# An encoder layer's MLP in two phases through DRAM, with Strassen's seven products in the up-projection

## The chip, the cores and the metric

The kernel runs on one core of one Trainium2 chip. Five engines work in parallel, each through its own queue of instructions in a fixed order: TensorE (PE: matmuls and transposes; PEld is its weight load), VectorE (DVE), ScalarE (ACT), GpSimd (POOL) and SyncE (SP), which issues nearly all DMAs here. An instruction that waits for a semaphore holds up everything behind it on its engine. The metric is the device time of one execution in microseconds, less is better; the figure is the median of several runs.

## The reference

The layer takes 16 meta tokens and 2048 tokens of width 1024 through a mixer (attention beside a state-space model) and an MLP. The part that the change touches, in float32:

```python
h = h + rms_norm(mix @ w_out[i], g_post_mix[i])
m = rms_norm(h, g_pre_mlp[i]) @ w_mlp_up[i]          # 2048 x 1024 @ 1024 x 4096
m = jnp.square(jax.nn.relu(m)) @ w_mlp_down[i]       # 2048 x 4096 @ 4096 x 1024
h = h + rms_norm(m, g_post_mlp[i])
```

## The kernel before

Float32 accuracy comes from three matmuls in place of one. `split` (L118 to L120) makes of a float32 tensor a high part (an ACT cast, L119) and a low part (a DVE subtraction, L120), and every product is high x high + high x low + low x high. A matmul has 128 rows and 128 columns of weights and streams 512 columns.

The stages on PE: projections, then attention with the state-space model and the gated unit beside it (until about 1600 us), the output projection (16 tiles of 128 tokens) and the MLP from 1818 us to the end. The kernel is written in a tile framework that orders each engine's queue itself, by priorities, and sets the waits from the tiles' pools: a pool with one buffer makes the next writer wait for the last reader. DMAs on SP go round eight completion lanes, so that each also waits for the one eight before it.

Output projection, `out_tile` (L1177 to L1212): per tile 48 matmuls (`op`, L1196), scaled and added by ACT (`ot`, L1200) and DVE (`o`, L1201), a row norm (`rstd_of`, small GpSimd instructions L125, L126), the residual, and a write of the tile to DRAM (`HD`, L1208). For tiles 0 to 7 follow the norm before the MLP (`hn`, L1165 to L1167) and, two tiles later, eight transposes (`hT`, L1174) whose splits lie in SBUF as `hh`, `hl`. The scratch buffer `ot`/`jk` has one copy, so a tile's chain must end before the next tile's first `ot` can be written.

MLP: two halves of 1024 tokens (`ct`). For each 256 of the 4096 inner columns, `up` (L1242 to L1263) loads 512 KB of weights twice and splits them; PE makes 24 matmuls for each 128 columns x 512 tokens (L1257), ACT takes the Relu (L1260), DVE squares (L1261), and the result is split into `mh`, `ml`, which stay in SBUF. `d_load` (L1265 to L1277) fetches the down weights through one buffer (`draw`), and `down` (L1279 to L1294) multiplies the block that was made one step earlier, and adds it into the accumulator `acc` (DVE, L1294). Up blocks and down blocks alternate on PE, one step apart, so that neither waits. Tiles 8 to 15 are normalised and transposed within the MLP, at the end of the first half. `finish` does the last norm and writes the output.

Of the kernel before, what the change touches and what calls it, by code (L numbers as in the profile page):

```python
# [9 lines left out]
F32 = mybir.dt.float32  # L10
# [12 lines left out]
# 2*pi cut into parts of few bits, so that a whole number times a part is exact.  # L23
# [18 lines left out]
# 1 / 10000 ** (2 j / 32) as float32 arithmetic gives it  # L42
# [9 lines left out]
def hymba_layer_kernel(  # L52
# [41 lines left out]
    # per group of 16 channels: row 16 (7 - i) + h, column = chunk of 8 tokens; the meta tokens' two chunks apart  # L94
# [9 lines left out]
    HD = mk(dram, [NT, 128, D], "HD")  # L104

# [35 lines left out]
        # a -> a - 2 pi round(a / 2 pi), exactly but for the last rounding  # L141
# [59 lines left out]
    # w_ukv columns are per head [64 nope | 64 v]: kept as [nope of all heads | v of all heads]  # L201
# [47 lines left out]
    # the meta tokens come second  # L249
# [62 lines left out]
    def proj(t, xhl):  # L312
        rows = 128 if t < NT else NM
        # kv latent and shared rotary key
# [55 lines left out]
    def u_T(t, un):  # L370
        # u, feature-major, to its chunks
# [103 lines left out]
    # what the first head doesn't wait for  # L475
# [7 lines left out]
    # ------------------------------------------------------------------ attention: its pools  # L483
# [34 lines left out]
    def head_units(h):  # L518
        # loads and splits of a head's keys and values, in small steps
# [71 lines left out]
    def attend(n, side):  # L591
        # side: for each key tile, the small steps of other work that go with it
# [15 lines left out]
        for t in range(NK):  # L608
# [12 lines left out]
            else:  # L621
                # rows 0..: high parts, 32..: low parts, 64..: high parts
# [23 lines left out]
    # the last queries' projections, beside the first maxima  # L646
# [11 lines left out]
    # ------------------------------------------------------------------ S5  # L658
# [23 lines left out]
    def exp_exact(pool, a, tag):  # L682
        # (exp(a), exp(a) - 1), both to float32's accuracy
# [33 lines left out]
    def s5_params():  # L717
        with pool("s5a", 1, "right") as ap:
# [60 lines left out]
            # exp(a) cos - 1 = (exp(a) - 1) - 2 exp(a) sin(half)^2, exp(a) sin = 2 exp(a) sin(half) cos(half)  # L779
# [11 lines left out]
            # (lam_bar - 1) / lam  # L791
# [22 lines left out]
            # powers  # L814
# [21 lines left out]
    def s5_all():  # L836
        yield from s5_params()
        s5z = s5.enter_context(pool("s5z", 1, "right"))
        # S5 states before each chunk: forward rows in rising, backward rows in falling order of chunks
# [38 lines left out]
            # C lam^n: forward rows n = 0..8, backward rows n = 8..0  # L878
# [21 lines left out]
        for b in range(NB5):  # L900
# [5 lines left out]
            for gg in range(S5B):  # L906
# [12 lines left out]
                # lags: forward 0..7 in slots 7..14, backward 7..0 in slots 0..7  # L919
# [11 lines left out]
                if gg == 1:  # L931
                    # two groups side by side in column tiles
# [283 lines left out]
    for t in range(NT):  # L1216
        nxt = operands(t + 1) if t + 1 < NT else None
        hn = out_tile(t, ops)
        if last and last[0][0] == t - 2:
            hn_T(*last.pop(0))  # L1220
# [146 lines left out]
```

## Time and profile before

| | |
|---|---|
| three runs | 3228.26, 3229.64, 3230.37 us, median 3229.64 |
| profiled execution: span | 3227.4 us |
| granted PE clock, mean | 0.982 |
| output projection's first matmul to the MLP's first | 1586.0 to 1818.2 us |
| MLP on PE | 1818.2 to 3219.6 us |

The page of the profile gives the busy time of each engine, 40 equal slices of the span, the chain of work that ended last, and the costliest groups of instructions. Other views give instructions in time, groups by line, and busy times in chosen windows. A line number in them is that of the kernel listed above, and a name like `up<-hh,uh` is output and inputs. In a group's row the numbers behind the bar are total busy us and mean ns of one, then the engine's idle time before them and what ended it.

### The profile page before, as it was taken

The page shows a single profiled execution, that of the slowest core. Times are in us where ns is not written, and L with a number is a line of the kernel's source. Part 1 is how long each engine was busy: PE and PEld are TensorE (multiplying, and loading weights), DVE is VectorE, ACT ScalarE, POOL GpSimd, SP SyncE. Part 2 cuts the span into 40 slices and gives each one's busy share as a digit, 9 for nine tenths or more (in the row PEclk, how much of TensorE's full clock was granted, in tenths as well). Part 3 has the DMA queues.
Part 4 walks back from the last instruction along what each step waited for, and adds up shares of the span by engine and source line. Part 5 has one row for each costly group of instructions (what it writes and reads, how often), then busy time and mean ns, then how long its engine had stood idle before and what let it go on. Part 6 is the DMA issues. An engine that isn't in the chain of part 4 may idle for free.

```text
span 3227.4 us, 41607 instructions
## 1 busy us (share of the span) xinstructions
PE 3097.5 (96%) x14839; PEld 2480.8 (77%) x14839; DVE 1863.1 (58%) x2943; ACT 1477.8 (46%) x2735; POOL 911.1 (28%) x2107
## 2 busy tenths in 40 slices
PE   6999988989999999999889999999999999999999
PEld 6899955656777766688767888888888888888887
DVE  6333278767888866675367534444446644444445
ACT  4333356988777799964444331122113422111122
POOL 4222166775888876600023100000000100000001
PEclk8999999999999999999989999999999999999999
DMA  4232231211000122231245411111112411111113
GB/s 150 64 85 75 64 82 30 59 43 31 26 14 26 26 73 85 68 122 46 71 133 141 150 47 45 52 52 49 50 46 79 157 52 46 53 46 46 46 46 104
DMA packets 228495, 216.52 MB, mean 67 GB/s; under 512 B 32336, under 2 KB 193488, under 8 KB 228288
## 3 DMA queue, kind: packets, MB, share of 16 engines
q1 hardware_dynamic: 226240, 212.17, 22.3%
q8 instruction: 116, 1.90, 0.2%
q10 hardware_dynamic: 1792, 1.57, 0.2%
q14 instruction: 91, 0.75, 0.1%
q0 software_dynamic: 256, 0.14, 0.0%
HBM read 160.34 MB, written 53.41 MB: 66 GB/s over the span
## 4 chain that ended last, share of the span: by engine, by line
PE 65%; ACT 4%; DMA 3%; issue 2%; DVE 2%; POOL 1%; SPq 0%; DVEq 0%; POOLq 0%; ACTq 0%
PE dn L1289 22%; PE up L1257 22%; PE z L1072 2%; PE s L612 2%; PE s L614 2%; PE s L613 2%; PE X L604 2%; PE X L605 2%; PE X L606 2%; PE mxp L566 2%; PE op L1196 2%; ACT zh L119 1%; DMA rb<-RD 1%; PE y L1008 1%; ACT ph L616 1%
## 5 line engine op out<-in xcount | busy, mean ns | idle before, releaser
L1294 DVE TENSOR_TENSOR acc<-dn,acc 128x512 f32<-128x512 f32 x464 | 316.9, 690 | 223.5 <-PE dn L1289 223.4
L620 DVE TENSOR_TENSOR pl<-s,ph 128x512 fp32r<-128x512 f32 x512 | 350.2, 686 | 160.2 <-ACT s L619 157.1
L616 ACT ACTIVATE ph<-s 128x512 fp32r<-128x512 f32 (+1 forms) x544 | 323.4, 595 | 171.1 <-PE s L614 155.9
L1257 PE MATMUL up<-hl,uh 128*128 128x512 f32 x1024 | 398.6, 389 | 0.0
L1257 PE MATMUL up<-hh,uh 128*128 128x512 f32 x1024 | 398.5, 389 | 0.0
L1257 PE MATMUL up<-hh,ul 128*128 128x512 f32 x1024 | 398.4, 389 | 0.0
L1289 PE MATMUL dn<-dh,ml 128*128 128x512 f32 x1008 | 392.3, 389 | 0.0
L1289 PE MATMUL dn<-dl,mh 128*128 128x512 f32 x1008 | 392.2, 389 | 0.0
L1289 PE MATMUL dn<-dh,mh 128*128 128x512 f32 x1008 | 392.0, 390 | 0.0
L567 DVE TENSOR_REDUCE mx<-mxp 128x1 f32<-128x512 f32 x512 | 343.0, 684 | 58.1 <-PE mxp L566 54.7
L119 ACT CAST dh<-raw 128x1024 fp32r<-128x1024 f32 x63 | 66.2, 1051 | 642.0 <-PE dn L1289 495.7
L125 POOL TENSOR_SCALAR rs_v<-ss 128x1 f32<-128x1 f32 (+1 forms) x98 | 24.3, 248 | 995.9 <-ACT hn L1165 662.8
L619 ACT ACTIVATE s<-s 128x512 f32<-128x512 f32 x512 | 304.0, 594 | 0.8
L612 PE MATMUL s<-ql,kh 96*128 96x512 f32 (+1 forms) x544 | 226.1, 416 | 14.3 <-ACT ZS L930 4.9
L1261 DVE TENSOR_TENSOR r<-r 128x512 f32<-128x512 f32 x128 | 88.3, 690 | 247.5 <-ACT r L1260 247.5
L604 PE MATMUL X<-pl,vt 128*65 128x512 f32 x512 | 208.9, 408 | 21.3 <-DVE pl L620 20.7
L1257 PEld LDWEIGHTS up<-hh,ul 128*128 128x128 f32 x1024 | 192.3, 188 | 40.1
L1257 PEld LDWEIGHTS up<-hl,uh 128*128 128x128 f32 x1024 | 192.2, 188 | 39.9
L1257 PEld LDWEIGHTS up<-hh,uh 128*128 128x128 f32 x1024 | 192.2, 188 | 39.9
L1289 PEld LDWEIGHTS dn<-dl,mh 128*128 128x128 f32 x1008 | 189.3, 188 | 39.4
L1289 PEld LDWEIGHTS dn<-dh,ml 128*128 128x128 f32 x1008 | 189.2, 188 | 39.5
L1289 PEld LDWEIGHTS dn<-dh,mh 128*128 128x128 f32 x1008 | 189.2, 188 | 39.2
(411 smaller groups left out, 6799.1 us busy)
## 6 DMA issues: line engine op xcount, KB each, us to landing
raw<-in_w_mlp_up_dram SPq DMA_DIRECT2D x64, 512.0 KB
raw<-in_w_mlp_down_dram SPq DMA_DIRECT2D x64, 512.0 KB
xt<-in_x_dram SPq DMA_DIRECT2D x32, 512.0 KB
ht<-HD SPq DMA_DIRECT2D x24, 512.0 KB
ug<-UD SPq DMA_DIRECT2D x32, 256.0 KB
HD<-o SPq DMA_DIRECT2D x16, 512.0 KB
out_dram<-jk SPq DMA_DIRECT2D x32, 256.0 KB
kvraw<-QD SPq DMA_DIRECT2D x32, 192.0 KB
```

Source lines behind the costliest of these rows:

```text
L119: S.copy(out=h, in_=src)
L566: T.matmul(out=p, lhsT=qs[n][0][0:96, j * 128:(j + 1) * 128], rhs=kh[0:96, b * 512:(b + 1) * 512])
L567: V.reduce_max(out=mxs[n][:, j, b:b + 1], in_=p, axis=AX.X)
L604: T.matmul(out=X[:65], lhsT=v[:, t, 0:65], rhs=pl_, start=(t == 0), stop=False)
L612: T.matmul(out=s[:m], lhsT=kh[0:96, cs], rhs=ql, start=True, stop=False)
L616: S.activation(out=ph_[:m], in_=s[:m], func=AF.Exp, scale=SCALE)
L619: S.activation(out=s, in_=s, func=AF.Exp, scale=SCALE)
L620: V.tensor_tensor(out=pl_, in0=s, in1=f(ph_), op=ALU.subtract)
L1257: T.matmul(out=p, lhsT=a[:, k], rhs=c[:, k, cs], start=(k == 0 and i == 0), stop=(k == 7 and i == 2))
L1261: V.tensor_tensor(out=r, in0=r, in1=r, op=ALU.mult)
L1289: T.matmul(out=p, lhsT=a[:, ts_], rhs=c[:, hs], start=(n == 0 and w == 0), stop=(n == len(keys) - 1 and w == 2))
L1294: V.tensor_tensor(out=acc[:, i, hs], in0=p, in1=acc[:, i, hs], op=ALU.add)
```

## The change

The MLP is done in two phases. Phase 1 makes the whole up-projection of all 2048 tokens, takes the squared Relu and stores it in DRAM (`MD`, 32 MB of float32). Phase 2 reads it back and does the whole down-projection.

In phase 1 the product of 256 inner columns and 1024 tokens (a pair) is seen as 2 x 2 blocks: 1024 input features in halves, columns in halves of 128, tokens in halves of 512. Strassen's algorithm (in Winograd's form) makes the four output blocks with seven block products instead of eight, and sums of blocks before and after. A block product is 12 matmuls.

- The token side's sums (`B11`, `B21`, `B22`, `T1` to `T4`) are made once per half of the tokens, in `hn_T`, on the transposed tiles: DVE makes `t1`, `t3`, GpSimd `t2` and `T4`. They are written to DRAM (`TBD`) per 128 tokens, in runs of 512 bytes, 256 KB each: two writes for a tile i < 4 of a half, two reads and five writes for one with i >= 4. `hn` is now made for all 16 tiles in the output projection, and transposed one tile later.
- `t_load` brings each of the seven back, 1 MB, through one buffer (`traw`) and splits it into `T{n}h`, `T{n}l`. For the first half that is done before the first pair, for the second within pair 15, after each of its products; the places of `T{n}` are the same for both halves.
- The weight side's sums are made per pair by GpSimd (`up_prep`), from a load of 1 MB, and split into a pool of nine places.
- The sums behind the products: two products are added onto others in PSUM (`first=False`), the rest goes by `p1`, `u2`, `u3` on ACT and DVE. The square moves from DVE to ACT.
- Phase 2 takes blocks of 512 inner columns, four parts of 512 tokens each; `m_load` fetches and splits the stored part, `d_load` the weights; the accumulator holds all 16 tiles.

The core of the diff (comments that the change removes and loads that stay alike are left out):

```diff
-        if t < 8:
-            hn = W["e1"].tile([128, D], F32, tag="hn", name="hn", bufs=2)
-            hn_norm(o, hn, jk)
-            return hn
+        hn = W["e1"].tile([128, D], F32, tag="hn", name="hn", bufs=2)
+        ss = sm.tile([128, 1], F32, tag="ss", name="ss")
+        S.activation(out=jk, in_=o, func=AF.Square, accum_out=ss)
+        r = rstd_of(ss, D)
+        V.scalar_tensor_tensor(out=hn, in0=o, scalar=r, in1=gpr, op0=ALU.mult, op1=ALU.mult)
+        return hn
...
+        if i < 4:
+            for n, p in ((B11, ps[0]), (B21, ps[1])):
+                b = t4(f"b{n}")
+                S.copy(out=b, in_=p)
+                put(n, b)
+        else:
...
+            S.copy(out=b22, in_=ps[1])
+            V.tensor_tensor(out=t1, in0=ps[0], in1=b11, op=ALU.subtract)
+            V.tensor_tensor(out=t3, in0=b22, in1=ps[0], op=ALU.subtract)
+            G.tensor_tensor(out=t2, in0=b22, in1=t1, op=ALU.subtract)
+            G.tensor_tensor(out=b21, in0=t2, in1=b21, op=ALU.subtract)
+            for n, b in ((B22, b22), (T1, t1), (T3, t3), (T2, t2), (T4, b21)):
+                put(n, b)
...
+        G.tensor_tensor(out=s1, in0=a21, in1=a22, op=ALU.add)
+        G.tensor_tensor(out=s2, in0=s1, in1=a11, op=ALU.subtract)
+        G.tensor_tensor(out=s3, in0=a11, in1=a21, op=ALU.subtract)
+        G.tensor_tensor(out=s4, in0=a12, in1=s2, op=ALU.subtract)
+        for src in (a11, s2, a12, s3, s1, a22, s4):
+            h = apool.tile([128, 4, 128], F32R, tag="ah", name="ah")
+            l = apool.tile([128, 4, 128], F32R, tag="al", name="al")
+            split(src, h, l)
+            yield h, l
...
+    def t_load(ct, n):
+        raw = tst.tile([128, 4, 512], F32, tag="traw", name="traw")
+        Y.dma_start(out=raw, in_=TBD[ct, n])
...
+        for k in range(0, 4, 2):
+            split(raw[:, k:k + 2], h[:, k:k + 2], l[:, k:k + 2])
...
+    def relu2(c, src, n, odd, half):
+        S.activation(out=c, in_=src, func=AF.Relu)
+        S.activation(out=c, in_=c, func=AF.Square)
+        ct, j = n // NP, n % NP
+        Y.dma_start(out=MD[ct, 2 * j + odd][:, half * 512:(half + 1) * 512], in_=c)
...
+        prod(pA, mine[0], TB[B11])
+        S.copy(out=p1, in_=pA)
+        step(0)
+        prod(pB, mine[1], TB[T2])
+        V.tensor_tensor(out=u2, in0=pB, in1=p1, op=ALU.add)
+        step(1)
+        prod(pA, mine[2], TB[B21], False)
+        relu2(rt(), pA, n, 0, 0)
+        step(2)
+        prod(pB, mine[3], TB[T3], False)
+        V.tensor_tensor(out=u3, in0=pB, in1=p1, op=ALU.add)
+        step(3)
+        prod(pE, mine[4], TB[T1])
...
+        prod(pF, mine[5], TB[T4])
...
+        prod(pE, mine[6], TB[B22], False)
...
-    mpool = ctx.enter_context(pool("mD", 4, "right"))
-    dpool = ctx.enter_context(pool("dD", 3, "right"))
-    draw = ctx.enter_context(pool("draw", 1, "right"))
-    acc = mk(accp, [128, 8, 1024], "acc")
+    mpool = ctx.enter_context(pool("mD", 8, "right"))
+    dpool = ctx.enter_context(pool("dD", 8))
+    draw = ctx.enter_context(pool("draw", 2))
+    acc = mk(accp, [128, NT, 1024], "acc")
...
+            raw = draw.tile([128, 512], F32, tag="mraw", name="mraw")
+            Y.dma_start(out=raw, in_=MD[c // 2, b * FB + q][:, (c % 2) * 512:(c % 2) * 512 + 512])
```

Three places in the engines' queues. First PE from the last output tile to the MLP, before: the last matmuls of the output projection, and the first of up, whose inputs `hh`, `hl` were split long ago (`woh`, `wol` are the output projection's weights).

```order
L1196 MATMUL op_20873<-wol_16801,sh_20722 128x512
L1196 MATMUL op_20873<-woh_16800,sl_20723 128x512
L1257 MATMUL up_20932<-hh_19056,uh_20926 128x512
L1257 MATMUL up_20932<-hh_19056,ul_20927 128x512
L1257 MATMUL up_20932<-hl_19057,uh_20926 128x512
```

The same place on PE now: the transposes of tiles 14 and 15 stand between, and the first product reads `T0h`, an operand that comes back from DRAM.

```order
L1186 MATMUL op_21113<-wol_16803,sh_20926 128x512
L1186 MATMUL op_21113<-woh_16802,sl_20927 128x512
L1221 MATMUL hT_21147<-ident_82,hn_21019 128x128 x4
L1221 MATMUL hT_21152<-ident_82,hn_21019 128x128 x4
L1221 MATMUL hT_21213<-ident_82,hn_21139 128x128 x4
L1221 MATMUL hT_21218<-ident_82,hn_21139 128x128 x4
L1303 MATMUL pA_21314<-T0h_21260,ah_21185 128x512
```

Nothing of up stands ahead of the last tile's transposes any more. Second, PE further on, at the end of pair 0's fifth product (`pE`) and the beginning of pair 1 (`pA_21465`).

```order
L1303 MATMUL pE_21316<-T4l_21293,ah_21201 128x512
L1303 MATMUL pE_21316<-T4h_21292,al_21202 128x512
L1303 MATMUL pF_21317<-T5h_21300,ah_21205 128x512
L1303 MATMUL pA_21465<-T0h_21260,ah_21344 128x512
L1303 MATMUL pA_21465<-T0l_21261,ah_21344 128x512
```

One matmul that reads operand 5 stands ahead of pair 1, which reads operands 0 and 1 first. Third, SP at the start of phase 1: `t1` to `b2` are tile 15's five writes (L1215), `traw` the operands' loads (L1290), the `MD` rows pair 0's results, `raw` a weight load.

```order
L1215 DMA TBD_80<-t1_21228 512x1x128
L1290 DMA traw_21258<-TBD_80 128x2048
L1215 DMA TBD_80<-b22_21227 512x1x128
L1215 DMA TBD_80<-t3_21230 512x1x128
L1215 DMA TBD_80<-t2_21229 512x1x128
L1215 DMA TBD_80<-b2_21224 512x1x128
L1290 DMA traw_21266<-TBD_80 128x2048
L1290 DMA traw_21274<-TBD_80 128x2048
L1290 DMA traw_21282<-TBD_80 128x2048
L1314 DMA MD_81<-r_21377 128x512
L1290 DMA traw_21290<-TBD_80 128x2048
L1251 DMA raw_21636<-in_w_mlp_up_dram 128x8x256
```

Before, SP held at that place the loads of down weights and of the MLP's residual, with nothing of the hidden state; now the first load of an operand stands behind the last tile's first write. At the end of phase 1 SP holds the first loads of phase 2 behind the last store.

```order
L1314 DMA MD_81<-r_26159 128x512
L1386 DMA raw_26188<-in_w_mlp_down_dram 128x1024
L1396 DMA mraw_26194<-MD_81 128x512
L1386 DMA raw_26200<-in_w_mlp_down_dram 128x1024
L1396 DMA mraw_26206<-MD_81 128x512
```

In before there was no such seam: up and down alternated.

More of the change, by code (lines that the diff above doesn't have):

```diff
@@ new lines, in hymba_layer_kernel, with up_prep @@
+    NP = FF // 256
+    def up_prep(n):
+        j = n % NP
+        raw = wraw.tile([128, 8, 256], F32, tag="raw", name="raw")
+        Y.dma_start(out=raw, in_=w_mlp_up[0, :, j * 256:(j + 1) * 256].rearrange("(k p) f -> p k f", p=128))
+        a11, a12, a21, a22 = raw[:, 0:4, 0:128], raw[:, 4:8, 0:128], raw[:, 0:4, 128:256], raw[:, 4:8, 128:256]
+        st = [wraw.tile([128, 4, 128], F32, tag=f"st{i}", name=f"st{i}", bufs=1) for i in range(4)]
+        s1, s2, s3, s4 = st
+        G.tensor_tensor(out=s1, in0=a21, in1=a22, op=ALU.add)
[7 more added lines that the diff above has]
+            yield h, l
@@ new lines, in hymba_layer_kernel, with prod @@
+    upr = up_.enter_context(pool("upr", 6, "right"))
+    TB = {}
+    def t_load(ct, n):
+        raw = tst.tile([128, 4, 512], F32, tag="traw", name="traw")
+        Y.dma_start(out=raw, in_=TBD[ct, n])
+        h = mk(tb, [128, 4, 512], f"T{n}h", F32R)
+        l = mk(tb, [128, 4, 512], f"T{n}l", F32R)
+        for k in range(0, 4, 2):
+            split(raw[:, k:k + 2], h[:, k:k + 2], l[:, k:k + 2])
+        TB[n] = (h, l)
+    def prod(p, left, right, first=True):
+        ah, al = left
+        bh, bl = right
+        for k in range(4):
+            for i, (a, b) in enumerate(((ah, bh), (ah, bl), (al, bh))):
+                T.matmul(out=p, lhsT=a[:, k], rhs=b[:, k], start=(first and k == 0 and i == 0),
+                         stop=(k == 3 and i == 2), skip_group_check=not first)
@@ new lines, in ut, with up_pair, step, rt @@
+    def ut(name):
+        return upu.tile([128, 512], F32, tag=name, name=name)
+    def relu2(c, src, n, odd, half):
[3 more added lines that the diff above has]
+        Y.dma_start(out=MD[ct, 2 * j + odd][:, half * 512:(half + 1) * 512], in_=c)
+    def up_pair(n):
+        ct = n // NP
+        mine = facs[:]
+        facs.clear()
+        nxt = up_prep(n + 1) if n + 1 < 2 * NP else iter(())
+        def step(i):
+            f = next(nxt, None)
+            if f is not None:
+                facs.append(f)
+            if n == NP - 1:
+                t_load(1, i)
+        def rt():
+            return upr.tile([128, 512], F32, tag="r", name="r")
+        pA, pB, pE, pF = pa("pA"), pa("pB"), pa("pE"), pa("pF")
+        p1, u2, u3 = ut("p1"), ut("u2"), ut("u3")
+        prod(pA, mine[0], TB[B11])
[11 more added lines that the diff above has]
+        prod(pE, mine[4], TB[T1])
+        r = rt()
+        V.tensor_tensor(out=r, in0=pE, in1=u3, op=ALU.add)
+        relu2(r, r, n, 1, 1)
+        step(4)
+        prod(pF, mine[5], TB[T4])
+        r = rt()
+        V.tensor_tensor(out=r, in0=u3, in1=pF, op=ALU.subtract)
+        relu2(r, r, n, 1, 0)
+        step(5)
+        prod(pE, mine[6], TB[B22], False)
+        r = rt()
+        V.tensor_tensor(out=r, in0=pE, in1=u2, op=ALU.add)
+        relu2(r, r, n, 0, 1)
+        step(6)
@@ new lines, in finish, with down @@
+            Y.dma_start(out=ov[t // 8, t % 8][:, hs], in_=jk[:, hs])
+    def down(b, t, ms, ds):
+        ts_ = slice((t % 4) * 128, (t % 4) * 128 + 128)
+        for half in range(2):
+            hs = slice(half * 512, (half + 1) * 512)
+            p = pa("dn")
+            for q in range(FB):
+                mh, ml = ms[q]
+                dh, dl = ds[q]
+                for w, (a, c) in enumerate(((mh, dh), (mh, dl), (ml, dh))):
+                    T.matmul(out=p, lhsT=a[:, ts_], rhs=c[:, hs], start=(q == 0 and w == 0),
+                             stop=(q == FB - 1 and w == 2))
+            if b == 0:
+                S.copy(out=acc[:, t, hs], in_=p)
+            else:
+                V.tensor_tensor(out=acc[:, t, hs], in0=p, in1=acc[:, t, hs], op=ALU.add)
@@ new lines, in hymba_layer_kernel @@
+    parts = [(b, c) for b in range(NB) for c in range(4)]
+    ds, ms = [], []
+    for d, m in zip(d_load(0), m_load(0, 0)):
+        ds.append(d)
+        ms.append(m)
+    nds = []
+    for n, (b, c) in enumerate(parts):
+        nm = m_load(*parts[n + 1]) if n + 1 < len(parts) else iter(())
+        if c == 0:
+            nd = d_load(b + 1) if b + 1 < NB else iter(())
+        nms = []
+        for i in range(4):
+            t = 4 * c + i
+            down(b, t, ms, ds)
+            if b == NB - 1:
+                finish(t)
+            nms.extend(x for x in [next(nm, None)] if x)
+            if i == 1:
+                nds.extend(x for x in [next(nd, None)] if x)
+        ms = nms
+        if c == 3:
+            ds, nds = nds, []
```

155 lines of the change are left out of this document (56 added, 99 removed).

## The prediction

> **What bounds the kernel now.** I read the page first: busy time, the slices, the chain that ended last.
>
> ```profile
> span 3227.4 us, 41607 instructions
> PE 3097.5 (96%) x14839; PEld 2480.8 (77%) x14839; DVE 1863.1 (58%) x2943; ACT 1477.8 (46%) x2735; POOL 911.1 (28%) x2107
> PE   6999988989999999999889999999999999999999
> PE 65%; ACT 4%; DMA 3%; issue 2%; DVE 2%; POOL 1%; SPq 0%; DVEq 0%; POOLq 0%; ACTq 0%
> ```
>
> TensorE is the busiest engine, and the last 18 slices, from 1775 us on, hold the MLP and read 9. A busy PE alone doesn't say that nothing else ends last, so the chain of waits from 1600 us on comes next (start, length, what).
>
> ```profile
> 1806.89 11.30 PE op L1196 x48
> 1818.20 43.57 PE up L1257 x192
> 1861.77 21.77 PE dn L1289 x96
> 1883.54 21.77 PE up L1257 x96
> ...
> 2471.33 0.87 PE hT L1174 x8
> 2472.20 2.76 PE dn L1289 x12
> ...
> 3175.40 44.15 PE dn L1289 x192
> 3219.57 0.70 DVE acc L1294
> ```
>
> Every piece from 1818.20 to 3219.57 is a matmul, each starting where the one before ended: the MLP is 1401.4 us of TensorE without a hole. 21.77 / 96 = **0.2268 us per matmul**, the price that a matmul taken away returns. (The page's 389 ns per matmul is start to end of one in a pipeline, which overlaps the next.) The other resources have room there, as the table of windows shows (PE, PEld, DVE, ACT, POOL busy, then clock, DMA share, GB/s):
>
> ```profile
> 2000.00:2600.00 600.00, 600.00 (x2679) 497.14 (x2678) 306.71 (x418) 150.24 (x238) 19.53 (x36) 1.00 0.22 67
> 1640.00:1660.00 20.00, 13.42 (x56) 10.60 (x55) 14.62 (x19) 8.55 (x16) 3.99 (x8) 0.83 0.49 154
> 1680.00:1740.00 60.00, 58.69 (x284) 48.00 (x282) 46.73 (x61) 31.11 (x55) 17.43 (x38) 1.00 0.53 147
> 2060.60:2062.40 1.80, 1.80 (x10) 1.49 (x9) 0.00 (x0) 0.00 (x0) 0.00 (x0) 1.00 0.87 280
> 2072.60:2074.90 2.30, 2.30 (x12) 1.91 (x11) 0.16 (x1) 0.60 (x1) 0.00 (x0) 1.00 0.77 223
> ```
>
> So what is taken from PE in the MLP comes back in full, unless the new form makes PE wait. PE is dense in before because everything it reads there already lies in SBUF; the sum below is about the places where the change sends it through DRAM.
>
> **1. Matmuls removed: -87.1 us.** Up had 2 halves x 32 x 2 x 24 = 3072 matmuls; seven products of 12 per pair, 32 pairs, make 2688. 384 x 0.2268 = 87.1. Down keeps 3072. A pair is 84 matmuls, 19.05 us, a product 2.72 us.
>
> **2. The steady pair: 0.** What stands beside those 19.05 us, priced by these groups (busy, mean ns):
>
> ```profile
> L119 ACT CAST mh<-r 128x512 fp32r<-128x512 f32 x128 | 79.2, 619 | 67.8 <-DVE r L1261 67.8
> L1260 ACT ACTIVATE r<-up 128x512 f32<-128x512 f32 x128 | 76.2, 595 | 284.8 <-PE up L1257 284.8
> L120 DVE TENSOR_TENSOR ml<-r,mh 128x512 fp32r<-128x512 f32 x128 | 88.1, 689 | 42.6 <-ACT mh L119 42.6
> L860 POOL TENSOR_TENSOR ul<-ug,uh 128x516 fp32r<-128x516 f32 x32 | 42.2, 1319 | 35.3 <-ACT uh L859 19.3 <-PE s L614 4.7 <-issue 4.6
> ```
>
> ACT: 7 casts, 8 activations, 1 copy, 16 x about 0.6 = 9.7 us. DVE: 12 x 0.69 = 8.3. GpSimd: 4 x 1.32 = 5.3. DMA: 1 MB in and 1 MB out, 2.1 MB / 19 us = 110 GB/s against the 280 shown. All lie beside PE. The third and fourth product are added onto pA and pB, so they wait for ACT's and DVE's reading of the first (about 0.7 us); at least one other product (2.72 us) stands between. Bounds: 0 to 1 us a pair, 0 to 32 in all; 0 taken, because cover is four times the wait.
>
> **3. Start of up: +50.** The seven operands come back from DRAM as 1 MB each through one buffer, and the next load is issued only when both splits of the last have read it. Before has such a single buffer in the down weights:
>
> ```profile
> 2059.58 6.05 SPq L1269 DMA_DIRECT2D raw<-in_w_mlp_down_dram  x2
> 2062.96 1.05 ACT L119 CAST dh<-raw 128x1024 fp32r<-128x1024 f32 x1 [4.87 <-DMA raw<-in_w_mlp_down_dram]
> 2064.04 1.23 DVE L120 TENSOR_TENSOR dl<-raw,dh 128x1024 fp32r<-128x1024 f32 x1 [4.48 <-ACT dh L119]
> ```
>
> 512 KB are there 3.38 us after the issue (2062.96 - 2059.58); another 512 KB at 280 GB/s add 1.87, so 5.25 for 1 MB. Then a cast (1.08 with its gap) and two subtractions (2 x 1.22): a **cycle of about 8.8 us** for one operand, against 2.72 us for the product that it feeds. PE runs products 1 to 5 as the operands come, and its order then holds one matmul of product 6, ahead of all of pair 1; it needs the first half of T5. From the first issue to there: 5 x 8.8 + 5.25 + 1.08 = 50.3 us, of which five products fill 13.6: 37 idle. From then on pair 1 covers the last operand. Between these loads SyncE also holds a write of m and a weight load of pair 3, and an operand queued behind them waits with them; they wait for products 3 and 4, done 2.72 us after their operand, plus two activations of 0.6, so 4 us into a cycle of 8.8: nothing added. Without that margin each such place would add what it lacks.
>
> Ahead of the first issue stands, in SyncE's order, the write of tile 15's t1. Its chain by these rows (tile 7's):
>
> ```profile
> 1729.92 1.03 PE L1174 MATMUL hT<-ident,hn 128*128 128x128 f32 x8
> ...
> 1734.27 0.33 SPq L1208 DMA_DIRECT2D HD<-o  x1
> 1734.28 1.06 ACT L1165 ACTIVATE jk<-o 128x1024 bf16<-128x1024 f32 x1 [1.20 <-DVE o L1207]
> 1736.72 2.57 POOL L126 TENSOR_TENSOR rs_r<-rs_v,mhalf 128x1 f32<-128x1 f32 x3
> 1737.61 1.28 DVE L1167 SCALAR_TENSOR_TENSOR hn<-o,rs_r,gpr 128x1024 f32<-128x1024 f32 x1
> 1737.82 0.69 ACT L1200 ACTIVATE ot<-op,rs_r 128x512 f32<-128x512 f32 x1 [1.87 <-POOL rs_r L126]
> ```
>
> After the last output matmul o takes 5.6 us (1818.20 to tile 15's HD write at 1823.76, row below), hn 4.6 (1738.89 - 1734.27), the transposes 1.0, t1 0.7: 12 us with PE nearly still, hidden in before since up starts on tiles long done. 37 + 12 = 49, with issue gaps 50. Bounds: 40 (a landing as short as for 512 KB, 1.9 x 5 less) to 62 (loads at 223 GB/s, as for rows of 512 B, and writes still under way in front of the first load).
>
> **4. Change of token half: +15.** Pair 15 reloads the seven operands in the same places; T0 lies ready in the buffer. Counted from the end of pair 15's first product, operand n is split 3.5 + 8.8 n us later (3.5 = 1.08 + 2 x 1.22), and its product in pair 16 is due at 16.3 + 2.72 n (six products, then n) plus earlier stalls: T3 29.9 against 24.5, T4 38.7 against 32.6, T5 47.5 against 41.4 with its first half 1.2 earlier. Late by 5.4, 6.1 and 4.9, of which I take 15; bounds 5 (half splits let the first matmuls go) to 35 (weight loads, 1 MB, in between on the same queue). After T5 pair 17 covers T6.
>
> **5. From up to down: +8.** The down tiles need pools in the place of up's operands, so their loads wait for the last product. SyncE holds the first down load behind the last write of m, and that behind an add (0.69) and two activations (1.2). Then 3.4 to land and 1.1 to cast: 6.4, and 1.6 more until the second weight and its m are split: 8. Bounds 6 (the first weight alone) to 20 (each of the first block's four weights waits 3.4 for its landing).
>
> **6. Output projection: +23.** Issues of HD by tile (tiles 3, 8, 15):
>
> ```profile
> 1679.51 0.34 SPq L1208 DMA_DIRECT2D HD<-o  x1
> ...
> 1748.06 0.46 SPq L1208 DMA_DIRECT2D HD<-o  x1
> ...
> 1823.76 0.32 SPq L1208 DMA_DIRECT2D HD<-o  x1
> ```
>
> Tiles with hn take (1748.06 - 1679.51) / 5 = 13.7 us, those without (1823.76 - 1748.06) / 7 = 10.8, which is PE's 48 x 0.2268. Now all sixteen have it: 7 x 2.9 = +20. Tiles 4 to 7 and 12 to 15 also put two GpSimd subtractions (1.32 each) on the queue that makes every row scale of the tile's serial chain (the POOL row above); half of the 2.6 counted, 8 x 1.3 = +10. The MLP loses its 8 x 0.87 us of transposes: -7. Sum 23. Bounds: +6 (the new chain hides in tiles already waiting) and +40: such a tile moves 3.7 MB, 12.7 us at 290 GB/s (223 / 0.77 of the row of 512-byte runs) but 16.5 at 223, and then DMA would set the tile. I take the chain, the nearer rows.
>
> **7. Ahead of that: +5.** Two weight loads of 1 MB, eight GpSimd sums (10.6 us) and nine splits stand among the first output tiles, where PE waits already (13.42 of 20 us busy at 1640). Bounds 0 to 12.
>
> **Sum:** -87.1 + 0 + 50 + 15 + 8 + 23 + 5 = +13.9 on the profiled execution's 3227.4 span: 3241.3. The median of the runs, 3229.64, lies 2.2 above that span, so **3243.5 us**.
>
> **A rule that speaks against the change.** In the window at 1640 PE has gaps and the granted clock is 0.83; in the gapless MLP it is 1.00. The Trainium skill, "TensorE: Matmul & The Clock Gate", section "HAM oscillation — how this bites in real kernels", says that a wait of over about 3.4 us puts the array back to half clock, so that each short burst behind it starts cold. The direction agrees with these two rows. By that page each re-warming costs about 1.7 us; the cold products of the start would hide in an 8.8-us cycle, and three places would add some 5 us: 3248.
>
> **Rivals.**
> *The chains hide (not slower).* The scheduler may move hn, transposes and writes into PE time of the next tile, so that a tile stays at PE's 11.9 us (48 matmuls and 1.0 of transposes). Decides: whether one tile's serial chain is under 11.9. Price: 16 x 11.9 = 190 against 13.7 x 8 + 10.8 x 8 = 196, so -6, and -7 from the MLP: term 6 would be -13 in place of +23, 36 less, 3207. With term 4 at its lower bound too, 3197; where half of the tiles do so, 3224. For it: 31 of 60 us of ACT and 47 of DVE busy in the window at 1680. Against: 13.7 us a tile with those engines idle half the time shows a chain, not a load. 0.25.
> *Transfers bind.* The 512-byte writes and read-backs collide: tiles 4 to 7 and 12 to 15 at 16.5 us add 8 x 1.5 above mine, and the first operand waits for them; or each pair stalls 1 us (+32). 3262 to 3300. For it: DMA share 0.53 in that stage before. Against: 110 GB/s in the pairs. 0.22.
> *Loads are ahead of PE.* All gain returns: 3229.64 - 87.1 = 3142.5; needs operands ready before PE does. Against: one buffer, and the last tile's t1 in front. 0.03.
>
> **How the numbers follow.** The forecast, 3224 to 3262, has 0.50. A measurement of this kernel can tell about 0.2%, 6.5 us: the bounds are 3223.2 and 3236.1. Faster holds the first and third rival, 0.27; same is the low part of the forecast, 0.18; the rest, 0.55, is slower. The term bounds at their ends would give 3200 to 3341, but not all stand at one end at once; the range 3200 to 3290 leaves out the third rival and the far end of the second.
>
> **What would show it.** A hole in PE of some 37 us between the first products, filled with five bursts of 12, with its releaser ACT or DVE splits L122/L123 of T1 to T5; three holes of 4 to 6 us in pairs 16 and 17; one of about 8 at the first down matmul; HD issues 13 to 15 us apart for all tiles. Between them pairs of 19.05 us without holes. Wrong if the operand cycle isn't 8.8 us, if pairs are longer than 19.1, or if output tiles come each 11 or each 17 us.

## The result, and the profile after

The changed kernel takes 3278.09 us (median of 4 runs, 3278.04 to 3278.12) against 3229.68 for the kernel before in the same session: ratio 1.0148, 95% interval 1.0134 to 1.0163. That is 48.4 us slower; 13.9 were forecast. The time lies inside the range 3200 to 3290, but above the 3224 to 3262 that had the chance of 0.50; the direction is the forecast one, and the size is more than three times the forecast. One execution of a kernel below (b_op256) took 8361 us at a granted clock of 0.37 and is left out of the ratio given for it.

The page of the changed kernel, to be read against the one above: 384 matmuls fewer, and still a longer span.

```profile
span 3276.3 us, 42280 instructions
PE 3064.8 (94%) x14455; PEld 2422.7 (74%) x14455; DVE 1797.9 (55%) x2875; ACT 1633.6 (50%) x3043; POOL 1099.7 (34%) x2251
PE   6999988989999999999689689998999899999999
PE 40%; DMA 2%; DVE 1%; ACT 1%; issue 0%; POOL 0%; SPq 0%; DVEq 0%; POOLq 0%; ACTq 0%
```

PE's row of slices has the holes that were looked for, near 1860 us, 2220 and 2550. The chain of waits at these places (start, length, what):

```profile
1862.59 6.27 DMA traw<-TBD
...
1868.96 1.05 ACT T0h L122
...
1870.04 2.37 DVE T0l L123 x2
...
1872.43 4.84 DMA traw<-TBD
...
1914.87 4.34 PE pA L1303 x12
...
1924.81 2.80 PE pA L1303 x12
...
2237.02 4.90 DMA traw<-TBD
...
2243.84 3.88 PE pA L1303 x12
...
2540.28 2.80 PE pE L1303 x12
...
2545.55 5.05 DMA raw<-in_w_mlp_down_dram
...
2552.24 147.76 PE dn L1428 x626
```

The cycle of load, cast and two subtractions stands there as forecast: from the issue at 1862.59 to the next at 1872.43 it is 9.8 us, later 8 to 10. The seam to phase 2, from the last product's end at 2543.08 to 2552.24, is 9.2 us. But a product without a wait takes 2.80 us (12 matmuls), not 2.72. The windows show the same over long stretches (the number in brackets behind PE's time is its instructions); first the kernel before, then the changed one:

```profile
2300.00:2400.00 100.00, 100.00 (x443) 82.79 (x442) 49.41 (x68) 17.08 (x24) 0.00 (x0) 1.00 0.16 48
2700.00:3000.00 300.00, 300.00 (x1325) 248.38 (x1324) 143.10 (x193) 57.72 (x81) 0.00 (x0) 1.00 0.16 50
```

```profile
2300.00:2400.00 100.00, 100.00 (x432) 81.06 (x432) 44.95 (x64) 49.50 (x86) 30.21 (x22) 1.00 0.35 111
2700.00:3000.00 300.00, 300.00 (x1293) 243.22 (x1292) 122.38 (x173) 45.29 (x67) 0.00 (x0) 1.00 0.20 67
```

PE is busy for the whole window in both kernels and the granted clock is 1.00 in both, yet it starts 1293 matmuls in 300 us in place of 1325: 0.2320 us from one to the next against 0.2264 (counted to the window's edges; the trace's own starts give 0.2324 and 0.2268). The second window holds down, whose instructions the change doesn't alter in kind. A busy share of 100% hides this.

With that the 48.4 us can be put together. The windows of the matmuls of L1303 alone (PE, PEld, clock, DMA share, GB/s) in the changed kernel give the stalls and up's cadence:

```profile
1848.30:1924.80 76.50, 37.27 (x98) 26.18 (x99) 0.69 0.50 165
2193.30:2253.20 59.90, 49.49 (x195) 38.35 (x194) 0.91 0.60 196
1950.00:2190.00 240.00, 240.00 (x1031) 193.07 (x1030) 1.00 0.33 108
2255.00:2540.00 285.00, 285.00 (x1228) 231.12 (x1227) 1.00 0.30 99
```

| part | forecast | measured, and how |
|---|---|---|
| 384 matmuls removed, at before's price | -87.1 | -87.1 |
| the other 5760 at a new price | 0 | +33: up 0.0064 x 1344 + 0.0057 x 1344 (240 / 1031 and 285 / 1228 less 300 / 1325), down 0.0056 x 3072 |
| start of up | +50 | +54: 76.5 less 98 x 0.2268 |
| change of half | +15 | +16: 59.9 less 195 x 0.2268 |
| up to down | +8 | +9 |
| output projection, with what stands ahead | +28 | +23: its last matmul ends at 1848.2 in place of 1818.2, less the MLP's 7 of transposes |
| sum | +13.9 | +48 |

Every stall is within 5 us of its term. What is missing is one row: the price of the matmuls that stay. Two small things nearly cancel in the sum. The 293 matmuls of the two stall windows are priced twice (293 x 0.0056 = 1.6 us), and the first 16 down matmuls behind the seam, at a granted clock of 0.62, are in no row: they take 5.85 us (2552.24 to 2558.09) against 16 x 0.2324 = 3.72, so 2.1 more.

```profile
2552.24 3.78 PE L1428 MATMUL dn<-dh,mh 128*128 128x512 f32 x8 [9.18 <-ACT mh L122]
2555.82 2.43 PE L1428 MATMUL dn<-dl,mh 128*128 128x512 f32 x8
2558.09 1.79 PE L1428 MATMUL dn<-dh,ml 128*128 128x512 f32 x7
```

### The profile page after: what moved, and what is told of

It reads as the page before. It is cut to its first block, busy times and chain, and to the rows that moved or that the text cites. A ratio compares the mean times of both kernels' runs of the same rounds, so it can differ in the third digit from the quotient of the medians.

```text
span 3276.3 us, 42280 instructions
## 1 busy us (share of the span) xinstructions
PE 3064.8 (94%) x14455; PEld 2422.7 (74%) x14455; DVE 1797.9 (55%) x2875; ACT 1633.6 (50%) x3043; POOL 1099.7 (34%) x2251
## 5 line engine op out<-in xcount | busy, mean ns | idle before, releaser
L1428 PE MATMUL dn<-dh,mh 128*128 128x512 f32 x1024 | 403.5, 397 | 9.2 <-ACT mh L122 9.2
L122 ACT CAST mh<-mraw 128x512 fp32r<-128x512 f32 x128 | 79.4, 620 | 455.4 <-PE dn L1428 374.8
L1433 DVE TENSOR_TENSOR acc<-dn,acc 128x512 f32<-128x512 f32 x224 | 154.1, 689 | 257.7 <-PE dn L1428 257.7
L1412 POOL TENSOR_TENSOR ss<-s2f 128x1 f32<-128x1 f32 x16 | 11.2, 698 | 744.3 <-ACT jk L1409 744.3
L616 PE MATMUL s<-qh,kl 96*128 96x512 f32 (+1 forms) x544 | 218.0, 401 | 0.0
L617 PE MATMUL s<-qh,kh 97*128 97x512 f32 (+1 forms) x544 | 214.2, 400 | 1.1 <-DMA qh<-nm 1.1
L569 PE MATMUL mxp<-kh,qh 96*128 96x512 f32 x512 | 197.6, 406 | 15.2 <-DVE pl L623 8.1
L609 PE MATMUL X<-ph,vt 128*65 128x512 f32 x512 | 204.4, 399 | 0.0
L608 PE MATMUL X<-ph,vt 128*64 128x512 f32 x512 | 204.3, 399 | 0.0
L122 ACT CAST ah<-st 128x512 fp32r<-128x512 f32 x128 | 79.1, 619 | 177.7 <-PE pB L1303 71.3
L615 PEld LDWEIGHTS s<-ql,kh 96*128 96x128 f32 (+1 forms) x544 | 104.1, 191 | 62.4 <-DVE mx L570 8.2
```

Of the source, the lines that this page charges most:

```text
L608: T.matmul(out=X[:64], lhsT=v[:, t, 65:129], rhs=ph_, start=False, stop=False)
L609: T.matmul(out=X[:65], lhsT=v[:, t, 0:65], rhs=ph_, start=False, stop=False)
L615: T.matmul(out=s[:m], lhsT=kh[0:96, cs], rhs=ql, start=True, stop=False)
L616: T.matmul(out=s[:m], lhsT=kl[:, cs], rhs=qh[0:96], start=False, stop=False)
L617: T.matmul(out=s[:m], lhsT=kh[:, cs], rhs=qh, start=False, stop=True)
L1428: T.matmul(out=p, lhsT=a[:, ts_], rhs=c[:, hs], start=(q == 0 and w == 0), stop=(q == FB - 1 and w == 2))
```

## The experiments

The runs come from five sessions, in which the median of the kernel before lies between 3229.38 and 3230.63 us; a difference between kernels of two sessions is good to about 1 us.

### What makes each matmul slower

The slow cadence is there in pairs and in down, beside 111 GB/s and beside 67, and its rhythm of a few matmuls doesn't follow the operands' names. (By the same count it is 0.2328 us in the first half's pairs and 0.2321 in the second's; that small difference stays unexplained.) In before the output projection has the slow cadence and the MLP the fast one, at the same clock. What the two have in common with the changed kernel's slow and fast places is where the tiles lie. In the built programs the start addresses of a matmul's moving operand and of its weights, in bytes of a partition, lie this far apart modulo 512:

```
before   up (hh, uh) 0     down (dh, mh) 0      output projection (woh, ah) 32
after    up (T, ah)  128   down (dh, mh) 384    output projection (woh, ah) 32
```

Hence theory A, that this distance sets the cadence, and four kernels that change nothing but places. An unused tile under the left-hand pools of the changed kernel:

```diff
     hx, hq = ExitStack(), ExitStack()
+    padp = ctx.enter_context(pool("padp", 1))
+    mk(padp, [128, 32], "pad")
```

> The changed kernel with an unused tile of 128 bytes per partition laid under the left-hand pools of the MLP, nothing else. It moves ah, al, dh, dl so that the start addresses of a matmul's weights and of its moving operand agree modulo 512 bytes, as they do in before's MLP (there the difference is 0; in the changed kernel it is 128 in up and 384 in down). Theory A (the distance of the two operands in SBUF sets the time from one matmul to the next): 0.2268 us instead of 0.2325 to 0.2333 in up and down, so 5760 x about 0.006 = 33 us less, 3245 us; the stalls at the start (54 us), at the change of half (15) and before down (9) stay. Rival B (the slower cadence comes from more DMA and ScalarE traffic, or from the products' waits): 3278 us, cadence unchanged. Rival C (the rhythm is set by chance after a stall): cadence differs between the three dense stretches.

Measured: 3247.39 us, 30.7 less than the changed kernel. The windows at the same places:

```profile
2300.00:2400.00 100.00, 100.00 (x443) 82.84 (x442) 45.62 (x65) 49.63 (x86) 27.01 (x20) 1.00 0.38 121
2700.00:3000.00 300.00, 300.00 (x1326) 248.39 (x1325) 129.07 (x180) 48.82 (x70) 0.00 (x0) 1.00 0.23 76
```

443 and 1326 matmuls, the cadence of before, with more DMA and ScalarE traffic than in the slow kernel: rivals B and C fall. The reverse in before:

```diff
+    padu = ctx.enter_context(pool("padu", 1))
+    mk(padu, [128, 32], "padu")
     wup = ctx.enter_context(pool("wup", 2))
...
+    padd = ctx.enter_context(pool("padd", 1, "right"))
+    mk(padd, [128, 32], "padd")
     dpool = ctx.enter_context(pool("dD", 3, "right"))
```

> The kernel before, with an unused tile of 128 bytes per partition between hh/hl and the up weights and another between the down weights and m, so that weights and moving operand lie 384 modulo 512 bytes apart; no instruction changes. Theory A: the MLP's cadence goes from 0.2268 to about 0.2325 us, 6144 x 0.0057 = 35 us more, 3265 us. Rivals B and C: 3230 us, since traffic, waits and stalls are those of before.

Measured: 3266.70 us, ratio 1.0117 (1.0102 to 1.0132), with the same number of instructions on PE, VectorE, ScalarE and GpSimd (14839, 2943, 2735 and 2107). Its windows:

```profile
2300.00:2400.00 100.00, 100.00 (x431) 80.42 (x430) 45.62 (x61) 19.75 (x29) 0.00 (x0) 1.00 0.15 48
2700.00:3000.00 300.00, 300.00 (x1293) 243.22 (x1292) 139.39 (x187) 58.74 (x83) 0.00 (x0) 1.00 0.16 50
```

The very 1293 of the changed kernel, in the kernel before. Two other sizes of the unused tile in the changed kernel (96 and 16 in place of 32 elements) tell the period:

> As the first, with 384 bytes: the operands lie 256 modulo 512 bytes apart. If what counts is the distance modulo 256 (or less), 0.2268 us and 3245; if modulo 512, a slow cadence of 0.232 to 0.234 and about 3278 us.

> As the first, with 64 bytes: 64 and 448 bytes apart modulo 512. If what counts is the distance modulo 64, 0.2268 us and 3245 (then the 128 and 384 of the changed kernel would have been fast, which they are not, so not expected); under theory A with 256 or 512, a slow cadence, about 3278 us. It shows whether the price depends on the distance.

Measured: 3248.58 and 3270.45 us (one execution each). Distance 256 is as fast as 0 (first row), and 64 in up and 448 in down are not (the second kernel's two rows):

```profile
2700.00:3000.00 300.00, 300.00 (x1326) 248.39 (x1325) 129.24 (x181) 48.83 (x70) 0.00 (x0) 1.00 0.23 76
```

```profile
2300.00:2400.00 100.00, 100.00 (x439) 82.06 (x438) 44.99 (x64) 49.61 (x86) 27.15 (x20) 1.00 0.36 118
2700.00:3000.00 300.00, 300.00 (x1288) 240.49 (x1287) 126.36 (x177) 48.30 (x70) 0.00 (x0) 1.00 0.22 73
```

So 0 modulo 256 is fast; 64 costs about a third of the full price (439), 128 and 192 cost all of it.

The address of one operand alone would be a rival, since each unused tile moves addresses too. The built programs rule it out. Modulo 512, moving operand and weights lie at 352 and 352 in before's up and at 480 and 480 in the 128-byte kernel, which are fast, but at 480 and 352 in the changed kernel's up and at 352 and 480 in its down, which are slow: each address stands in a fast and in a slow place, for either operand.

In the output projection the same move:

```diff
+        po = ph.enter_context(pool("padO", 1, "right"))
+        mk(po, [128, 56], "padO")
         ip = W["ip"] = ph.enter_context(pool("iO", 2, "right"))
```

> The kernel before with an unused tile of 224 bytes per partition above the output projection's operands, so that its weights and moving operand lie 256 in place of 32 bytes apart modulo 512. Theory A with a period of 256: the output projection's cadence goes from 0.2333 to 0.2268 us, 5 us over its 768 matmuls where PE is the bound (tiles 8 to 15 at 10.8 us a tile) and nothing where the chain is: 2.5 us of 3230, at the edge of what can be timed, while the cadence in the trace tells it plainly. Rivals: cadence 0.2333.

Measured: 3230.37 us, ratio 1.0002 (0.9993 to 1.0011): nothing, which fits a stage that isn't set by PE's pace alone. The cadence that this edit gives is read from a later kernel that has it too (a_order_op, below).

### The start of up and the change of half

On the 128-byte kernel, two buffers for the operands' loads:

```diff
-    tst = up_.enter_context(pool("tst", 1, "right"))
-    upr = up_.enter_context(pool("upr", 6, "right"))
+    tst = up_.enter_context(pool("tst", 2, "right"))
+    upr = up_.enter_context(pool("upr", 5, "right"))
```

> The 128-byte kernel (3247) with two buffers for the operands' loads (traw) and five in place of six for r, to make room. Theory (the start and the change of half are set by the serial cycle load, cast, two subtractions of one buffer, 8.8 us): a cycle near 4.4 to 5 us, the ten holes at the start and the five at the change of half shrink to a third, about 20 us at the start and 14 at the change, 3210 to 3216 us. Rival (the loads are bound by DMA or by the SP queue and not by the buffer): cycle stays near 8 us, under 8 us gained, 3240 or more.

Measured: 3219.38 us, 28.0 less and 0.9965 of before (0.9951 to 0.9979): faster than the kernel before. The holes between products at the change of half are all but gone; in the window there PE is busy throughout, where it was 49.5 of 59.9 us:

```profile
2170.00:2230.00 60.00, 59.24 (x262) 48.78 (x261) 44.85 (x52) 41.95 (x66) 17.61 (x12) 1.00 0.61 211
```

The theory of the single buffer holds; the time is 3 us above the upper end of what was expected. In its trace the first load went out later (1870.6 in place of 1865.4) and the seam to down grew (13.6 us in place of 9.1); no run separates the two. Next the order in which the right-hand places are given out:

```diff
-    tb = up_.enter_context(pool("tb", 1, "right"))
     tst = up_.enter_context(pool("tst", 2, "right"))
+    tbs = [up_.enter_context(pool(f"tb{n}", 1, "right")) for n in range(7)]
...
-        h = mk(tb, [128, 4, 512], f"T{n}h", F32R)
-        l = mk(tb, [128, 4, 512], f"T{n}l", F32R)
+        h = mk(tbs[n], [128, 4, 512], f"T{n}h", F32R)
+        l = mk(tbs[n], [128, 4, 512], f"T{n}l", F32R)
```

> The two-buffer kernel (3219) with the right-hand places given out in another order: the buffers of the operand loads and T0 first, which puts them on the output projection's weights instead of on the last tile's xt, ot and hn. Theory (the 25 us from the last output matmul to the first of up are a chain of o, hn, transposes and t1 that the loads wait for only because they take that tile's places and stand behind its writes): the first three loads go out before the last tile's chain ends, the seam falls from 25 to 8 to 12 us, 3203 to 3209. Rival (the loads wait for the writes of the last tile or for DMA): seam above 20 us, 3216 to 3220.

Measured: 3204.74 us, ratio 0.9919 (0.9904 to 0.9934). The time is the forecast one, the seam isn't: it is 17.7 us, not 8 to 12. The rows of SyncE and PE (start, length, what, and in brackets the idle time before and its releaser):

```profile
1848.47 0.80 SPq L1292 DMA_DIRECT2D traw<-TBD  x2
...
1860.34 0.33 SPq L1200 DMA_DIRECT2D HD<-o  x1
```

```profile
1848.52 1.06 PE L1223 MATMUL hT<-ident,hn 128*128 128x128 f32 x8
1864.73 1.94 PE L1223 MATMUL hT<-ident,hn 128*128 128x128 f32 x8 [15.14 <-DVE hn L1206]
1866.32 0.78 PE L1305 MATMUL pA<-T0h,ah 128*128 128x512 f32 x1
```

Two loads now go out 12 us before the last tile's HD write, and their operands are ready; what PE waits for is hn of tile 15, whose transposes stand ahead of pair 0 in its queue. The seam gave 7.7 of the 14.6 us (25.3 to 17.7); the rest came from the holes between the first products and from the seam to down (11.2 in place of 13.6). With the output projection's places moved as well:

> The same with 224 bytes more above the output projection's operands, so that its weights and moving operand lie 256 instead of 32 bytes apart modulo 512. Cadence of the output projection 0.2268 in place of 0.2333 by theory A; time 0 to 4 us less than without it, since that stage waits for its chain.

Measured: 3207.06 us, the same within the runs' spread. Its last output matmuls stand 0.2268 us apart ((1852.59 - 1849.64) / 13):

```profile
1849.64 0.39 PE L1190 MATMUL op<-wol,ah 128*128 128x512 f32 x1
...
1852.59 0.39 PE L1190 MATMUL op<-woh,sl 128*128 128x512 f32 x1
```

The distance rule holds there too (0.2333 before), and the stage gains nothing by it.

### The output projection

Two edits on the 128-byte kernel: `V.tensor_tensor` for `G.tensor_tensor` at t2 and T4, and a tag of its own for `jk`.

```diff
-            G.tensor_tensor(out=t2, in0=b22, in1=t1, op=ALU.subtract)
-            G.tensor_tensor(out=b21, in0=t2, in1=b21, op=ALU.subtract)
+            V.tensor_tensor(out=t2, in0=b22, in1=t1, op=ALU.subtract)
+            V.tensor_tensor(out=b21, in0=t2, in1=b21, op=ALU.subtract)
```

> The 128-byte kernel with the two subtractions t2 and T4 of the output projection on VectorE in place of GpSimd. If they hold up the row scales on GpSimd, as the prediction's sixth term had it with 10 us for eight tiles, the output stage gets 5 to 12 us shorter: 3236 to 3242. If the tile's chain has room for them, no change beyond 3 us: 3245 to 3250.

```diff
-        jk = W["e1"].tile([128, 512], F32, tag="ot", name="jk").bitcast(BF16)
+        jk = W["e1"].tile([128, 512], F32, tag="jk", name="jk").bitcast(BF16)
```

> The 128-byte kernel with a buffer of its own for the squares' scratch jk, which shared one copy with ot. If the tile's chain through this buffer sets the 13 to 15 us of a tile, the stage gets 1 to 2 us a tile shorter, 16 to 30 us in all: 3218 to 3232. If the chain through the row scales (o, its norm, hn's norm) sets it, under 5 us: 3243 to 3248.

Measured: 3249.19 and 3248.31 us, no gain by either. And hn for all sixteen tiles in the kernel before, which tests the sixth term's main cause alone:

```diff
-        if t < 8:
-            hn = W["e1"].tile([128, D], F32, tag="hn", name="hn", bufs=2)
-            hn_norm(o, hn, jk)
-            return hn
+        hn = W["e1"].tile([128, D], F32, tag="hn", name="hn", bufs=2)
+        hn_norm(o, hn, jk)
+        return hn if t < 8 else None
```

> The kernel before with hn made for all sixteen tiles in the output projection; for tiles 8 to 15 nothing reads it, and they are normalised again within the MLP as before. If the serial chain of hn is what makes tiles longer (the sixth term: 7 x 2.9 = 20 us), the tiles 8 to 15 go from 10.8 to 13 to 14 us and the time to 3244 to 3252. If the writes and read-backs through DRAM or the transposes did it in the changed kernel, 3230 to 3236.

Measured: 3228.57 us, ratio 0.9996 (0.9987 to 1.0006). The last HD write goes out at 1832.6 us, 8.8 later than in before, and tiles 8 to 15 come 12.2 us apart in place of 10.8, but PE doesn't wait for it there: the last output matmul ends no later than in before. So the tiles' chain is longer by hn and costs PE nothing, as long as PE isn't made to wait for it. In the changed kernel it is; the group of the transposes in the output stage, whose last columns are the idle time of PE before them and its releaser:

```profile
L1221 PE MATMUL hT<-ident,hn 128*128 128x128 f32 x120 | 18.6, 305 | 41.5 <-DVE hn L1204 41.5
```

41.5 us before transposes, which the change put one tile behind in place of two; 23.7 of it is one wait, before tile 0's at 1644.91. Undone in the changed kernel, and in the reordered one:

```diff
-        if last:
+        if last and last[0][0] == t - 2:
             hn_T(*last.pop(0))
...
-    hn_T(*last.pop(0))
+    while last:
+        hn_T(*last.pop(0))
```

> The changed kernel with the transposes of a tile two tiles behind its output projection, as before had them, in place of one; nothing else. In the changed kernel PE stood 41.5 us before transposes that waited for hn. Theory (the transposes stand in PE's queue ahead of the next tile's matmuls before hn is ready, and that is what lengthens the output stage): the stage from 262.8 us towards the 232 of before plus 8 of added transposes, 20 to 25 us less, 3253 to 3260. Rival (the stage is set by the chain of o, by DMA or SP, and the transposes wait only because PE has nothing else): under 5 us less, 3273 to 3279.

> The reordered kernel (3205) with the same edit. Theory: 20 to 25 us less, 3180 to 3186, though the last two tiles' transposes and writes now end later and the seam may grow by 1 to 4 us. Rival: 3200 to 3206.

Measured: 3274.60 us, 3.5 less than the changed kernel, and 3196.74, 8.0 less than the reordered one, 0.9898 of before (0.9881 to 0.9914). In the first PE's wait before transposes fell from 41.5 to 14.5 us:

```profile
L1221 PE MATMUL hT<-ident,hn 128*128 128x128 f32 x120 | 18.0, 290 | 14.5 <-DVE hn L1204 12.2 <-DVE o L1191 2.2 <-ACT ah L122 0.2
```

Of the 14.5 us, 8.4 already lie behind the last output matmul. The next rows are the stage from its first output matmul to its last (PE's busy time, and further on the granted clock), in before, in the changed kernel and with the lag of two tiles:

```profile
1586.00:1818.20 232.20, 208.04 (x906) 166.97 (x907) 143.09 (x184) 94.45 (x163) 52.00 (x112) 0.94 0.46 127
1585.50:1848.20 262.70, 214.00 (x954) 172.05 (x955) 159.01 (x193) 107.58 (x189) 85.98 (x146) 0.91 0.63 178
1584.80:1833.30 248.50, 221.85 (x948) 174.22 (x948) 156.94 (x188) 105.82 (x185) 85.54 (x136) 0.92 0.64 180
```

PE is idle 24.2, 48.7 and 26.6 us of it. So the lag of one tile made 22 of the 24.5 us of idle time that the stage gained. What it still has over before with the lag of two, 16.3 us, is 13.8 of busy time, with the transposes of six more tiles in it and a granted clock of 0.92 against 0.94, and 2.5 of idle time.

The last output matmul came 15 us earlier, and most of it was given back at the seam, which grew from 21.8 to 31.6 us: neither theory nor rival, but a wait that moved behind the stage. Phase 1 begins with the last tile's chain, and that ends only 5 us earlier (last HD write at 1851.2 in place of 1856.6). Two more tries at the chain, on the last kernel:

```diff
-            Y.dma_start(out=TBD[ct, n][:, :, cs], in_=src)
+            S.dma_start(out=TBD[ct, n][:, :, cs], in_=src)
```

> The reordered kernel with transposes two tiles behind (3197), with the writes of the transposed tiles and their sums issued by ScalarE's DMA queue in place of SyncE's. Theory (the writes stand in SyncE's one queue and hold up the loads of the next tiles' operands behind them while they wait for the sums): the tiles get 1 to 1.5 us shorter, the stage 10 to 25 us, 3172 to 3187. Rival (the stage is set by the tiles' own chain, or the writes now hold up ScalarE instead): 3193 to 3203.

```diff
-            Y.dma_start(out=b11, in_=TBD[ct, B11][:, :, cs])
-            Y.dma_start(out=b21, in_=TBD[ct, B21][:, :, cs])
+            S.copy(out=b11, in_=ps[0])
+            S.copy(out=b21, in_=ps[1])
```

> The same kernel as the base, without the two read-backs of b11 and b21 for tiles 4 to 7 and 12 to 15: copies of the tile's own transposes take their place, so this leaves out the sums over two blocks of tokens. If the read-backs (512 KB a tile, waiting for writes that have just gone out) set the tiles' time: 8 tiles x 1 to 2 us, 3181 to 3189. If not, 3193 to 3199.

Measured: 3197.33 and 3195.05 us (the second in one execution), no change. In the first's profile the last output matmul starts 5.0 us earlier (1826.4 in place of 1831.4), and the seam behind it is 2.0 longer (31.5 in place of 29.5). Neither the writes' place in SyncE's queue nor the read-backs set the time.

## Why the prediction was off

**The step that failed** is the price: "0.2268 us per matmul, the price that a matmul taken away returns", and then "Down keeps 3072", at no cost. It took the cadence of before for a property of the instruction. It is a property of the instruction and of where its two operands lie: pools with other sizes moved the up weights and the operands T from 0 to 128 bytes apart, the down weights and m from 0 to 384, and the 5760 matmuls that stay became 2.5% dearer, 33 us. A pair of 84 took 19.5 us, past the 19.1 that the prediction names as a sign of being wrong. Moving the tiles back returned 30.7 us, and moving before's tiles by the same 128 bytes cost it 37.1 (3266.70 less 3229.57). The trace of before held a sign: in rows that the prediction quotes, 48 matmuls of the output projection take 11.30 us and 96 of down 21.77, which is 0.2354 (by the starts 0.2333) against 0.2268 at a granted clock near 1.00, and the difference wasn't asked about. Term 6 even reads 10.8 us a tile as "PE's 48 x 0.2268", where 48 of the output projection's matmuls at 0.2333 are 11.2.

**Term 1, the count:** right, 2688 matmuls and 32 pairs.

**Term 2, the steady pair:** right that nothing in a pair waits; at equal places a product takes 2.72 us, as forecast.

**Terms 3 and 4, start and change of half:** right in mechanism and size, 50 against 54 and 15 against 16. The holes of pair 16 stand where they were forecast, before T3, T4 and T5, with 2.5, 5.2 and 2.8 us of idle PE; the rest of the 16 is matmuls at a lower clock and at the new price. The cycle of one buffer was 8 to 10 us, and a second buffer took 28 us off the time. The rule about the clock went the way that it was told: the 12 matmuls from 1914.87 on, behind bursts with rests of 2 to 4 us, took 4.34 us against 2.80 later, and the granted clock in the start's window is 0.69. For products 1 to 5 that hid in the cycle, since each was done before the next operand came. By the Trainium skill, "TensorE: Matmul & The Clock Gate", section "HAM oscillation — how this bites in real kernels", some 5 us more had been estimated for three places. The trace has 4.7 there that nothing hides: 1.5 behind the start's last wait (4.34 less 2.80), 1.1 behind that of the change of half (3.88 less 2.80) and 2.1 at the first down matmuls. That section counts only half of its 1.67 us at half clock as lost, where the prediction took about 1.7 for each place; the 1.1 to 2.1 measured are nearer to the prediction's figure.

**Term 5, up to down:** right, 8 against 9.

**Terms 6 and 7, the output projection:** the size was near, 28 against 23, by luck, since the main reason was wrong. Not the longer chain of hn as such lengthens the stage (it cost before nothing), nor GpSimd's subtractions, but PE waiting for that chain at transposes one tile behind: 22 us of idle time went with a lag of two tiles. Term 7 had the right kind of cause, 7.6 us at the first HD write (1636.07 against 1628.50) for 5: in GpSimd's queue the sums of pair 0's weights stand before tile 0's row scale, whose `rs_v` comes at 1628.29 in place of 1625.08, and the first of them waits for its load.

```profile
1624.66 1.27 POOL L1255 TENSOR_TENSOR st<-raw 128x512 f32<-128x512 f32 x1 [22.20 <-DMA raw<-in_w_mlp_up_dram]
1628.29 0.18 POOL L128 TENSOR_SCALAR rs_v<-ss 128x1 f32<-128x1 f32 x1
```

The scratch buffer, GpSimd's subtractions, the writes' queue and the read-backs were each taken away without effect on the time; what else sets a tile's 12 to 15 us stays open.

**The rivals:** transfers didn't bind in the pairs, the chains didn't hide, the loads weren't ahead. None of the three had the operands' places in it; the slower side of the range was reached by a cause that wasn't on the list. Two small sums of the prediction are off: the upper ends of the bounds give 3343.5 with the 2.2 us of the median, not 3341, and the first and third rival have 0.28 together, not 0.27.

What Strassen's algorithm is worth here appears when the rest is mended: with equal places, a second load buffer, the new order of places and two tiles of lag the same seven products take 3196.74 us, 33.0 less than before in that session; 87.1 were there to be had, and the seam from the output projection (29.5 us in that kernel) and the one to down (11) hold most of what is still missing.

## What to carry to other kernels

Take the time from one matmul's start to the next as something to be measured at each place, not as a constant: it is read by counting instructions in a window in which PE never rests, since busy share and granted clock don't show it. When a change gives pools other sizes, compare the start addresses of weights and moving operand before and after; here an unused tile of 128 bytes was worth 31 us. And where a step through DRAM replaces data that lay ready, its single buffer and the place of its first load in the queue decide whether the arithmetic saved arrives.

## What the runs showed of the hardware that was not expected

The time from one 128x512 matmul (operands cast to fp32r, each with its own weight load) to the next depends on the distance of the two operands' start addresses in SBUF. By the windows and the starts in the trace: 0.2268 us at 0 and 256 bytes modulo 512, 0.2324 to 0.2333 at 32, 128, 384 and 448, and 0.2289 at 64. Other distances were not tried, nor other types or widths; why the distance matters isn't shown by these runs.

Rests of 2 to 4 us between bursts of 12 matmuls are enough for the clock to fall. At the start of up PE rests 3.01 us before product 2, behind a stretch at full clock, and 2.30 us before the first half of product 6; the granted clock before the first rest, behind it and behind the second (the column after the last count):

```profile
1874.10:1877.40 3.30, 1.27 (x6) 0.70 (x4) 0.69 (x1) 1.22 (x3) 0.00 (x0) 1.00 0.67 281
1877.50:1884.20 6.70, 5.35 (x12) 3.76 (x12) 2.36 (x2) 1.78 (x2) 0.00 (x0) 0.50 0.35 114
1915.00:1918.40 3.40, 3.40 (x10) 2.63 (x9) 2.08 (x2) 1.42 (x3) 0.00 (x0) 0.50 0.31 96
```

Both rests are shorter than the 3.4 us of the prediction's rule, so that figure isn't the least that it takes here.

VectorE took longer where GpSimd read SBUF beside it (from the reordered kernel with two tiles of lag): the scaling of o takes 1.27 to 1.29 us in 13 tiles and 2.25 to 2.31 in three. In the one shown it starts beside GpSimd's subtraction and ends 1.08 us after that one did.

```profile
1754.11 1.32 POOL L1242 TENSOR_TENSOR t<-b,t 128x512 f32<-128x512 f32 x1 [3.81 <-ACT b L1239]
1754.26 2.25 DVE L1198 SCALAR_TENSOR_TENSOR o<-o,rs_r,gpo 128x1024 f32<-128x1024 f32 x1
1755.51 2.16 POOL L1243 TENSOR_TENSOR b<-t,b 128x512 f32<-128x512 f32 x1
```

The Trainium skill, "SBUF — State Buffer", section "SBUF: two separate sides", says that a VectorE instruction with two SBUF inputs and a GpSimd instruction that reads SBUF exclude each other for a whole instruction; these rows agree. What it costs the kernel was not measured.
